# Four edits to the order of a hybrid decoder step: all samples of a head at once, a block's end in pieces, later recurrences, shifted query weights

## The chip, the cores and the metric

The kernel runs on one core of a Trainium2 chip. The metric is the device time of one execution in microseconds; the median of the runs counts. A core has TensorE (PE, with its weight loads as PEld), VectorE (DVE), ScalarE (ACT), GpSimd (POOL) and SyncE (SP, which here only issues transfers). Transfers are issued from SP, ACT and POOL.

## The reference

One layer of a decoder trunk for a prompt of 2048 tokens and eight single-token samples that carry state. All is float32.

```python
hn = rmsnorm(x, g_norm) * (1 + scale) + shift            # scale, shift, gate from silu(c) @ w_ada + b_ada
xa, za, q, k, v, glr, zg = split(hn @ w_in)
xc = conv4(xa)                                           # RG-LRU group, 8 blocks of 128 channels
gx, ga = sigmoid(xc @ w_gate_x + b_x), sigmoid(xc @ w_gate_a + b_a)
a = exp(8 * ga * log_sigmoid(lambda));  u = sqrt(1 - a**2) * gx * xc
h_t = a_t * h_{t-1} + u_t;              y_lru = h * silu(za)
S_t = diag(alpha_t) S_{t-1} + k_t^T v_t;  o_t = q_t S_t  # gated linear attention, 4 heads, 128 x 256 state
y_gla = rmsnorm(o) * silu(zg)
y = rmsnorm(x + gate * (concat(y_lru, y_gla) @ w_out), g_final)
```

The samples take one step of each recurrence from their own states (`state_lru_h`, `state_lru_conv`, `state_gla`), and the new states are outputs, for the attention eight matrices of 128 x 256 per head.

## The kernel before

**Arithmetic.** A float32 projection is done as three products of rounded parts (high x high, high x low, low x high), all at the rate of one product each; `hh` and `hl` hold the high and low part of the normalized input `hn`, channels on the partitions. Every weight tile holds its high and low part (`weights`); parts that were made once are kept in device memory (`parts`) and loaded again for the second half.

**Stages.** The prompt is worked in two halves of 1024 tokens; `SEGS` cuts a half into segments of 512 and 512 (first half) or 384, 384 and 264 columns (second half, the last 8 being the samples).

1. Start: the modulation from `w_ada`, `hn` of the first half, and the values, keys and queries of the first head (head 3). The tiles of this stage lie in the pool `start`, the first head's query weights `wq` among them.
2. First half: for each head of `HEADS` = (3, 0, 1, 2) `gla_head` and then `lru` for the RG-LRU blocks of `LRU_TILES`, here (0), (1, 2), (3, 4), (5, 6, 7). The last block, 7, is done in `lru_last_a`, where the normalization of the second half (`next_hn`) is dealt out among its projections (`drips`).
3. Middle: `gates_ahead` and `gates_seven` for the gates of the second half and `lru_seven` for blocks 0 and 1, products of 2 x 2 blocks done as seven (`seven`). Their operands are sums of quarters of `hn`, made on VectorE and ScalarE by `sums`, again dealt out by `drips`, two per product.
4. Second half: `gla_head(1, h)` and one block of `LATE_TILES` after each head, then blocks 6 and 7 while the first operands of the output projection are made (`early`).
5. Output projection, residual and the final norm, in an order written out by hand.

**Order.** Within the program text, work that belongs later is queued with `after(units, fn)` on a heap and run by `tick`; a unit is one projection of 512 columns, a product of `seven` is half a unit. The queued functions of the attention are flagged `gla`, its chunks also `val`; `new_values` runs what is queued before the value tiles are taken again, `flush_gla` everything of the attention. What stands where in each engine's queue is then decided by a planner: it goes through the instructions by the order in which they were written and by its own estimate of when their inputs are ready and their tile is free. `behind(q)` places what it encloses behind the last instruction written on that engine. A tile of a pool is named by its tag; each tag has a fixed number of buffers, and a new tile waits for the last user of the buffer that it takes. Here this concerns `xt` (two of 1032 columns in `xp`), `wr` (two of 1088 columns in `wp`, for raw weights), `zs` (four of 512 columns, for gate values), and the single tiles of an RG-LRU block: `xa` (the convolution's input), `cv` (its output), `xl`, `tx` and `tg`.

**The attention's recurrence.** `gla_qk` makes the scaled query and key of a segment; `chunks` starts the recurrence (`gla_start`, two tiles of products and transposes) and goes on chunk by chunk; `finish` normalizes, turns (`gla_out`) and gates with `zs`. In the second half `sample_state` and `sample_out` do the samples of a head in two groups of four: load values `vb` and states `s0` into two `xt` tiles, scale by the decay (ScalarE), add the outer product (VectorE), multiply by the queries laid out in `qm` (TensorE, `po`, each sample on its own 32 columns of the array), and store the states.

**An RG-LRU block.** `xa_unit` projects and convolves, `gates` multiplies by the gate weights, takes the tanh and, with the last segment, goes on to the block's end: the exponentials and the root on ScalarE, three products and the scan on VectorE. `za_unit` makes the gate; `out` multiplies and stores to `mixd`, from which the output projection reads.

Of the kernel before, what the change touches and what calls it, by code (L numbers as in the profile page):

```python
# [8 lines left out]
F32 = mybir.dt.float32  # L9
# [5 lines left out]
P = 128  # L15
# [34 lines left out]
def dram(ap, off, pattern):  # L50
    return bass.AP(tensor=ap.tensor, offset=ap.offset + off, ap=pattern)
# [3 lines left out]
def hybrid_kernel(ctx, tc, i, o):  # L55
# [381 lines left out]
    with tc.tile_pool(name="ada", bufs=1, side="right") as ap:  # L437
# [263 lines left out]
    def after(units, fn, gla=False, val=False):  # L701
        clock[1] += 1
        heapq.heappush(pend, (clock[0] + units, clock[1], fn, gla, val))
# [8 lines left out]
            heapq.heappop(pend)[2]()  # L712

    def flush_gla():
        while any(e[3] for e in pend):
            e = min(e for e in pend if e[3])
            pend.remove(e)
            heapq.heapify(pend)
            e[2]()

    def ada_gate():

# [365 lines left out]
        for c in range(nch):  # L1088
            V.tensor_scalar(on[:, c], on[:, c], rs[:, c:c + 1], None, op0=OP.mult)

    def sample_state(h, smp, b0, st, done):

        if b0 == 0:
            st[:] = [cp.tile([P, NS, 32], F32, tag="sc", name="qm"), gp.tile([P, DV], F32, tag="os", name="os")]
            V.memset(st[0], 0.0)
        qm = st[0]
        vb = xp.tile([P, 4, DV], F32, tag="xt", name="xt")
        G.dma_start(vb, dram(vsd, (h * NS + b0) * DV, [[0, P], [DV, 4], [1, DV]]))
        s0 = xp.tile([P, 4, DV], F32, tag="xt", name="xt")
        G.dma_start(s0, i["state_gla"][0, b0:b0 + 4, h].rearrange("b k v -> k b v"))  # L1100
        for n in range(4):
            b = b0 + n
            V.tensor_copy(qm[:, b, b:b + 1], smp[:, 0, b:b + 1])
            S.activation(s0[:, n], s0[:, n], AF.Copy, scale=smp[:, 2, b:b + 1])  # L1104
            V.scalar_tensor_tensor(s0[:, n], vb[:, n], smp[:, 1, b:b + 1], s0[:, n],
                                   op0=OP.mult, op1=OP.add)
        after(3, lambda: sample_out(h, b0, st, s0, done), True)

    def sample_out(h, b0, st, s0, done):

        qm, os_ = st
        po = psum.tile([P, 512], F32, tag="o", name="po", bufs=1)[:, :DV]
        for n in (3, 0, 1, 2):
            PE.matmul(po[32 * n:32 * n + 32], qm[:, b0 + n], s0[:, n], start=True, stop=True)
        G.dma_start(o[7][0, b0:b0 + 4, h].rearrange("b k v -> k b v"), s0)
        if b0 == 0:
# [7 lines left out]
        V.tensor_scalar(os_, os_, rs[:, :1], None, op0=OP.mult)  # L1124
        done()

    def silu(z, ps):
        S.activation(z, ps, AF.Tanh, scale=0.5)  # L1128
# [41 lines left out]
    def gla_head(half, h, wv=None, ahead=None):  # L1170
# [4 lines left out]
        else:  # L1175
# [8 lines left out]
        prep, zs, os_, state = {}, {}, [None], []  # L1184

        def chunks(s, c):

# [31 lines left out]
        def sample(smp, b0):  # L1219
            sample_state(h, smp, b0, state, lambda: after(0.5, lambda: os_.__setitem__(0, state[1]), True))  # L1220

        pk = None
        if not wv:
# [38 lines left out]
    def lru_units(half, last_a=None, seven=False):  # L1262
# [40 lines left out]
                V.tensor_tensor(xl[:, c], cv[:, c], xh[:, c].bitcast(F32), op=OP.subtract)  # L1303

        def gates(t, ss):
            j, cv, xh, xl, wgh, wgl, res = t.j, t.cv, t.xh, t.xl, t.wgh, t.wgl, t.res
            if ss[0] == 0:
                t.tx, t.tg = t_("tx"), t_("tg")
            tx, tg = t.tx, t.tg
            for s in ss:  # L1310
                c0, sn = t.segs[s]
                c = slice(c0, c0 + sn)
                for g, (out, bias) in enumerate(((tx, hbx), (tg, hba))):
                    ps = acc()[:, :sn]
                    PE.matmul(ps, wgh[:, g], xh[:, c], start=True, stop=False)  # L1315
                    PE.matmul(ps, wgh[:, g], xl[:, c], start=False, stop=False)
                    PE.matmul(ps, wgl[:, g], xh[:, c], start=False, stop=True)
                    S.activation(out[:, c], ps, AF.Tanh, bias=bias[:, j:j + 1], scale=0.5)  # L1318
            if ss[-1] < len(t.segs) - 1:
                return  # L1320
            n_ = slice(0, TH + (NS if t.samples else 0))
            a = last_a() if last_a else t_("xl")
            S.activation(a[:, n_], tg[:, n_], AF.Exp, bias=lc2[:, j:j + 1], scale=lc2[:, j:j + 1])

            S.activation(tg[:, n_], tg[:, n_], AF.Tanh, bias=lc4[:, j:j + 1], scale=lc4[:, j:j + 1])
            S.activation(tg[:, n_], tg[:, n_], AF.Sqrt, scale=0.25)
            if half == 1 and j in LRU_TILES[3][:2]:

                S.activation(t.one, tg[:, :1], AF.Tanh)
            V.scalar_tensor_tensor(tx[:, n_], tx[:, n_], 1.0, cv[:, n_], op0=OP.add, op1=OP.mult)  # L1330
            V.scalar_tensor_tensor(tg[:, n_], a[:, n_], 1.0, tg[:, n_], op0=OP.add, op1=OP.mult)
            V.tensor_tensor(tx[:, n_], tx[:, n_], tg[:, n_], op=OP.mult)
            h = tg
            V.tensor_tensor_scan(h[:, pr], a[:, pr], tx[:, pr], 0.0 if half == 0 else hc[:, j:j + 1],  # L1334
                                 op0=OP.mult, op1=OP.add)
            if half == 0:
                V.tensor_copy(hc[:, j:j + 1], h[:, TH - 1:TH])
            else:
                V.tensor_copy(stT[:, j, 3:4], h[:, TH - 1:TH])
            if t.samples:  # L1340
                V.tensor_tensor(h[:, sm], a[:, sm], vecT[:, j, R_H0:R_H0 + NS], op=OP.mult)
                V.tensor_tensor(h[:, sm], h[:, sm], tx[:, sm], op=OP.add)
                V.tensor_copy(stT[:, j, 12:20], h[:, sm])
            res.append(h)

        def out(t, s, z):
            j, h = t.j, t.res
            if not h:
                after(1, lambda: out(t, s, z))
                return  # L1350
            c0, sn = t.segs[s]
            V.scalar_tensor_tensor(z, h[0][:, c0:c0 + sn], 0.5, z, op0=OP.mult, op1=OP.mult)
            spill(z, j, half, c0, sn)
# [24 lines left out]
        def xa_new(t):  # L1378
            t.xh = t_("xh", F32R, 48)
            t.one = lp.tile([P, 1], F32, tag="one", name="one")  # L1380
            t.xl, t.xa, t.cv = t_("xl", F32R), t_("xa", extra=8), t_("cv")
            if half == 0:
                V.memset(t.xa[:, :3], 0.0)
            else:
                V.tensor_copy(t.xa[:, :3], xac[:, t.j])
# [21 lines left out]
        def za_unit(t, s):  # L1407
            c0, sn = t.segs[s]
            z = xp.tile([P, 512], F32, tag="f512", name="z5") if half == 1 and t.j == LRU_TILES[3][0] and s == 2 else None
            z = silu2(t.wz, c0, sn, z)  # L1410
            after(2, lambda: out(t, s, z))
            tick()

        if seven:
            return xa_load, xa_new, xa_unit, out
        return xa_load, xa_unit, za_load, za_unit

    def lru(half, js, wx=None):
# [205 lines left out]
        seven(n, use, lambda s: new(), n == 0)  # L1624

    def lru_seven(j):
        xa_load, xa_new, xa_unit, out = lru_units(1, seven=True)
# [12 lines left out]

    def gates_ahead(h):

# [616 lines left out]
```

## Time and profile before

| | |
|---|---|
| runs | 1453.64, 1453.55, 1456.39 us (median 1453.64) |
| profiled execution | 1452.05 us |
| its span, first to last instruction | 1450.3 us |
| granted TensorE clock | 0.997 of full speed |
| busy: TensorE, weight loads, VectorE, ScalarE, GpSimd | 1425.6, 1253.1, 1051.2, 690.0, 220.5 us |
| transfers | 305.33 MB, 211 GB/s in the mean |

The profile is that of one execution; its own time, not the median, is what its rows add up to. A row of the timeline gives the start, the duration, engine, line, operation and tiles of one instruction or of a few merged ones (x), and in brackets the idle time of the engine before it and what ended it. `PE ... <- DVE ...` in the list of waits means that TensorE idled until that VectorE instruction was done. Matmuls overlap: a busy time of 0.39 us and a distance of 0.23 us to the next are both right.

### The profile page before, as it was taken

The page shows a single profiled execution, that of the slowest core. Times are in us where ns is not written, and L with a number is a line of the kernel's source. Part 1 is how long each engine was busy: PE and PEld are TensorE (multiplying, and loading weights), DVE is VectorE, ACT ScalarE, POOL GpSimd, SP SyncE. Part 2 cuts the span into 40 slices and gives each one's busy share as a digit, 9 for nine tenths or more (in the row PEclk, how much of TensorE's full clock was granted, in tenths as well). Part 3 has the DMA queues.
Part 4 walks back from the last instruction along what each step waited for, and adds up shares of the span by engine and source line. Part 5 has one row for each costly group of instructions (what it writes and reads, how often), then busy time and mean ns, then how long its engine had stood idle before and what let it go on. Part 6 is the DMA issues. An engine that isn't in the chain of part 4 may idle for free. (4 is left out here: it accounts for less than half of the span.)

```text
span 1450.3 us, 23579 instructions
## 1 busy us (share of the span) xinstructions
PE 1425.6 (98%) x8741; PEld 1253.1 (86%) x8741; DVE 1051.2 (72%) x2477; ACT 690.0 (48%) x1251; POOL 220.5 (15%) x364
## 2 busy tenths in 40 slices
PE   8999999999999999999999999999999999999998
PEld 6888989899898988878999998999998887788886
DVE  5757658776676688955458687686888986688886
ACT  4644544662545358624354544535557522144342
POOL 0200111212122013100111321433210000000000
PEclk9999999999999999999999999999999999999999
DMA  9755775774665446667844665756672767694453
GB/s 329 267 185 175 259 264 196 251 243 156 200 217 192 160 175 213 204 224 236 293 153 154 201 205 163 244 188 203 213 256 77 279 223 273 229 361 135 135 173 116
DMA packets 161752, 305.33 MB, mean 211 GB/s; under 512 B 12962, under 2 KB 91458, under 8 KB 159197
## 3 DMA queue, kind: packets, MB, share of 16 engines
q1 hardware_dynamic: 106837, 217.39, 44.0%
q0 software_dynamic: 22752, 70.44, 14.3%
q10 hardware_dynamic: 32048, 16.00, 3.7%
q8 instruction: 69, 1.13, 0.3%
q14 instruction: 46, 0.38, 0.1%
HBM read 188.51 MB, written 115.33 MB: 210 GB/s over the span
## 5 line engine op out<-in xcount | busy, mean ns | idle before, releaser
L661 PE MATMUL acc<-hh,w 128*128 128x512 f32 (+3 forms) x1112 | 386.2, 347 | 1.3 <-DVE zs L1129 0.7
L663 PE MATMUL acc<-hh,w 128*128 128x512 f32 (+3 forms) x1112 | 375.6, 338 | 0.0
L662 PE MATMUL acc<-hl,w 128*128 128x512 f32 (+3 forms) x1112 | 375.3, 338 | 0.2 <-DVE hl L205 0.2
L661 PEld LDWEIGHTS acc<-hh,w 128*128 128x128 f32 x1112 | 209.3, 188 | 20.0 <-ACT tx L1318 0.9
L662 PEld LDWEIGHTS acc<-hl,w 128*128 128x128 f32 x1112 | 209.3, 188 | 17.2 <-DVE hl L205 0.5
L663 PEld LDWEIGHTS acc<-hh,w 128*128 128x128 f32 x1112 | 209.1, 188 | 16.8 <-issue 0.4
L1845 PE MATMUL acc<-w,a 128*128 128x512 f32 (+1 forms) x792 | 184.8, 386 | 0.0
L1845 PEld LDWEIGHTS acc<-w,a 128*128 128x128 f32 x792 | 146.8, 188 | 33.2 <-issue 3.4
L346 PE MATMUL acc<-w,hh 128*128 128x256 f32 (+1 forms) x508 | 144.9, 285 | 0.1
L347 PE MATMUL acc<-w,hh 128*128 128x256 f32 (+1 forms) x508 | 143.6, 283 | 0.0
L348 PE MATMUL acc<-w,hl 128*128 128x256 f32 (+1 forms) x508 | 143.6, 283 | 0.0
L1845 PE MATMUL tp<-w,a 128*128 128x512 f32 x564 | 136.0, 391 | 0.0
L1845 PEld LDWEIGHTS tp<-w,a 128*128 128x128 f32 x564 | 105.3, 188 | 26.8 <-issue 5.2
L346 PEld LDWEIGHTS acc<-w,hh 128*128 128x128 f32 x508 | 96.8, 191 | 1.3 <-ACT zs L1128 0.4
L348 PEld LDWEIGHTS acc<-w,hl 128*128 128x128 f32 x508 | 96.4, 190 | 0.0
L347 PEld LDWEIGHTS acc<-w,hh 128*128 128x128 f32 x508 | 95.9, 189 | 0.2
L1128 ACT ACTIVATE zs<-acc 128x512 f32<-128x512 f32 (+3 forms) x70 | 34.5, 492 | 107.4 <-PE acc L663 105.2
L1695 ACT CAST a<-s 128x512 fp32r<-128x512 f32 x61 | 36.5, 619 | 95.9 <-issue 36.6
L1278 DVE SCALAR_TENSOR_TENSOR cv<-xa,vecT,cv 128x512 f32<-128x512 f32 (+2 forms) x120 | 77.1, 645 | 6.0 <-ACT cv L1276 5.7
L1129 DVE SCALAR_TENSOR_TENSOR zs<-zs,acc 128x512 f32<-128x512 f32 (+3 forms) x70 | 38.6, 551 | 47.3 <-ACT zs L1128 47.2
L957 ACT CAST vh<-acc 128x256 fp32r<-128x256 f32 x56 | 20.5, 370 | 83.3 <-PE acc L348 70.0
L958 DVE TENSOR_TENSOR vl<-acc,vh 128x256 fp32r<-128x256 f32 x56 | 23.4, 420 | 43.1 <-ACT vh L957 43.0
(403 smaller groups left out, 2752.0 us busy)
## 6 DMA issues: line engine op xcount, KB each, us to landing
parts<-w SPq DMA_DIRECT2D x37, 1024.0 KB
w<-parts SPq DMA_DIRECT2D x28, 1024.0 KB
wr<-in_w_in_dram SPq DMA_DIRECT2D x38, 512.0 KB
a<-mixd SPq DMA_DIRECT2D x63, 256.0 KB
w<-wd SPq DMA_DIRECT2D x12, 1024.0 KB
w<-twd SPq DMA_DIRECT2D x20, 512.0 KB
mixd<-zs ACTq DMA_DIRECT2D x34, 256.0 KB
wada<-in_w_ada_dram SPq DMA_DIRECT2D x16, 512.0 KB
```

The source lines that it names most:

```text
L346: PE.matmul(ps, hh[:, kt, c], hi[:, kt % 4], start=kt == 0, stop=False)
L347: PE.matmul(ps, hh[:, kt, c], lo[:, kt % 4], start=False, stop=False)
L348: PE.matmul(ps, hl[:, kt, c], hi[:, kt % 4], start=False, stop=kt == KT - 1)
L661: PE.matmul(ps[:, :n], hi[:, kt], a, start=kt == 0, stop=False)
L662: PE.matmul(ps[:, :n], hi[:, kt], b, start=False, stop=False)
L663: PE.matmul(ps[:, :n], lo[:, kt], a, start=False, stop=kt == KT - 1)
L958: V.tensor_tensor(lo, ps[:, :DV], hi.bitcast(F32), op=OP.subtract)
L1128: S.activation(z, ps, AF.Tanh, scale=0.5)
L1129: V.scalar_tensor_tensor(z, z, 1.0, ps, op0=OP.add, op1=OP.mult)
L1278: V.scalar_tensor_tensor(cv[:, cq], xa[:, cq.start + k:cq.stop + k], cw[k], cv[:, cq], op0=OP.mult, op1=OP.add)
L1695: S.copy(t[:, 0, k], (low(t) if src is None else src)[:, k])
L1845: PE.matmul(ps, t[:, u, k], w[:, v, k, c], start=(q < 3 or ps is own) and (k, u, v) == (0, 0, 0), stop=(k, u) == (3, 1), skip_group_check= ...
```

## The change

Four edits, independent in the code:

- **Query weights.** The tile of the first head's query weights gets 56 columns more, and the weights are placed behind them.
- **Recurrences.** In the first half the recurrence of heads 0, 1 and 2 starts two units after the first `gla_qk` instead of one (head 3 had two already). `flush_gla` sets the clock to the due time of what it runs, so that what is queued from there is queued from that time, and sets it back at its end.
- **The end of block 7 in the first half.** The end of a block becomes a list of four functions, `chain`: exponentials, root and first product; second product; third product; scan. They are run at once for every other block; for block 7 of the first half they are run 4.5, 5, 5.5 and 6 units after its gates, each behind the last VectorE and ScalarE instruction written by then. `out` looks for the result every half unit. The gate values of this block go into the columns of its `xa` tile instead of `zs` tiles. `lru_seven` fills the first columns of its `xa` only before its first sum into it (`xa_first`).
- **Samples.** `sample_state` loads and updates all eight samples, 0 to 3 in two `xt` tiles, 4 to 7 in two `wr` tiles; four units later (instead of three for each group) `sample_out` does all their matmuls, the second four added to the first in `po`, and stores. One copy takes the place of a copy and an add.

```diff
-        wkq0.append(weights(Q0 + HEADS[0] * DK, DK, both=st.tile([P, 2, D], F32R, name="wq"), later=True))
+        wkq0.append(weights(Q0 + HEADS[0] * DK, DK, both=st.tile([P, 2 * D + 56], F32R, name="wq")[:, 56:].rearrange("p (j n) -> p j n", j=2), later=True))
...
     def flush_gla():
+        now = clock[0]
         while any(e[3] for e in pend):
...
+            clock[0] = max(now, e[0])
             e[2]()
+        clock[0] = now
...
-    def sample_state(h, smp, b0, st, done):
...
+    def sample_state(h, smp, done):
+
+        qm = cp.tile([P, NS, 32], F32, tag="sc", name="qm")
+        V.memset(qm, 0.0)
+        s0 = []
+        for b0, pool, tag in ((0, xp, "xt"), (4, wp, "wr")):
+            vb, x = [pool.tile([P, 1088], F32, tag=tag, name=tag)[:, :4 * DV] if b0 else
+                     pool.tile([P, 4 * DV], F32, tag=tag, name=tag) for _ in range(2)]
+            vb, x = [y.rearrange("p (b v) -> p b v", v=DV) for y in (vb, x)]
+            G.dma_start(vb, dram(vsd, (h * NS + b0) * DV, [[0, P], [DV, 4], [1, DV]]))
+            G.dma_start(x, i["state_gla"][0, b0:b0 + 4, h].rearrange("b k v -> k b v"))
+            for n in range(4):
...
+            s0.append(x)
+        after(4, lambda: sample_out(h, qm, s0, done), True)
+
+    def sample_out(h, qm, s0, done):
+
+        os_ = gp.tile([P, DV], F32, tag="os", name="os")
         po = psum.tile([P, 512], F32, tag="o", name="po", bufs=1)[:, :DV]
-        for n in (3, 0, 1, 2):
-            PE.matmul(po[32 * n:32 * n + 32], qm[:, b0 + n], s0[:, n], start=True, stop=True)
-        G.dma_start(o[7][0, b0:b0 + 4, h].rearrange("b k v -> k b v"), s0)
-        if b0 == 0:
-            V.tensor_copy(os_, po)
-            return
-        V.tensor_tensor(os_, os_, po, op=OP.add)
+        for m in range(2):
+            for n in (3, 0, 1, 2):
+                PE.matmul(po[32 * n:32 * n + 32], qm[:, 4 * m + n], s0[m][:, n], start=m == 0, stop=m == 1)
+        for m in range(2):
+            G.dma_start(o[7][0, 4 * m:4 * m + 4, h].rearrange("b k v -> k b v"), s0[m])
+        V.tensor_copy(os_, po)
...
-                after(2 if h == HEADS[0] else 1, lambda: chunks(0, 0), True, True)
+                after(2 if half == 0 or h == HEADS[0] else 1, lambda: chunks(0, 0), True, True)
...
-            after(1, lambda: sample(prep[2][3], 0), True)
-            after(3, lambda: sample(prep[2][3], 4), True)
+            after(1, lambda: sample(prep[2][3]), True)
...
+            if half == 0 and j == LRU_TILES[3][-1]:
+
+                def late(ops):
+                    with behind(V), behind(S):
+                        ops[0]()
+                    if ops[1:]:
+                        after(0.5, lambda: late(ops[1:]))
+                after(4.5, lambda: late(chain(t)))
+            else:
+                for f in chain(t):
+                    f()
+
+        def chain(t):
...
+            return [rates, scale, inputs, scan]
...
-                after(1, lambda: out(t, s, z))
+                after(0.5 if half == 0 and j == LRU_TILES[3][-1] else 1, lambda: out(t, s, z))
...
+            if half == 0 and t.j == LRU_TILES[3][-1]:
+                z = t.xa[:, c0:c0 + sn]
...
-        seven(len(HEADS) - 1 + j, use, lambda s: t.xa[:, 3 + s * 512:3 + s * 512 + 512])
+        def c2(s):
+            if s == 0:
+                xa_first(t)
+            return t.xa[:, 3 + s * 512:3 + s * 512 + 512]
+
+        seven(len(HEADS) - 1 + j, use, c2)
```

More of the change, by code (lines that the diff above doesn't have):

```diff
@@ L1089, in gla_norm @@
             V.tensor_scalar(on[:, c], on[:, c], rs[:, c:c + 1], None, op0=OP.mult)
-    def sample_state(h, smp, b0, st, done):
-        if b0 == 0:
[L1094 to L1107, printed above, removed]
@@ L1109, in sample_out @@
[L1109 to L1119 removed]
+    def sample_state(h, smp, done):
[9 more added lines that the diff above has]
+            for n in range(4):
+                b = b0 + n
+                V.tensor_copy(qm[:, b, b:b + 1], smp[:, 0, b:b + 1])
+                S.activation(x[:, n], x[:, n], AF.Copy, scale=smp[:, 2, b:b + 1])
+                V.scalar_tensor_tensor(x[:, n], vb[:, n], smp[:, 1, b:b + 1], x[:, n],
+                                       op0=OP.mult, op1=OP.add)
+            s0.append(x)
+        after(4, lambda: sample_out(h, qm, s0, done), True)
@@ L1124, in sample_out @@
         V.tensor_scalar(os_, os_, rs[:, :1], None, op0=OP.mult)
-        done()
+        done(os_)
     def silu(z, ps):
@@ L1217, in finish, with sample @@
             gla_out(half, h, s, prep[s, "run"][1], os_[0] if s == 2 else None, [zs[s, 0], zs[s, 1]])
-        def sample(smp, b0):
-            sample_state(h, smp, b0, state, lambda: after(0.5, lambda: os_.__setitem__(0, state[1]), True))
+        def sample(smp):
+            sample_state(h, smp, lambda x: after(0.5, lambda: os_.__setitem__(0, x), True))
         pk = None
@@ L1321, in gates @@
             n_ = slice(0, TH + (NS if t.samples else 0))
             a = last_a() if last_a else t_("xl")
[L1323 to L1344, printed above, removed]
+            def rates():
+                S.activation(a[:, n_], tg[:, n_], AF.Exp, bias=lc2[:, j:j + 1], scale=lc2[:, j:j + 1])
+                S.activation(tg[:, n_], tg[:, n_], AF.Tanh, bias=lc4[:, j:j + 1], scale=lc4[:, j:j + 1])
+                S.activation(tg[:, n_], tg[:, n_], AF.Sqrt, scale=0.25)
+                if half == 1 and j in LRU_TILES[3][:2]:
+                    S.activation(t.one, tg[:, :1], AF.Tanh)
+                V.scalar_tensor_tensor(tx[:, n_], tx[:, n_], 1.0, cv[:, n_], op0=OP.add, op1=OP.mult)
@@ new lines, in scale, with inputs, scan @@
+            def scale():
+                V.scalar_tensor_tensor(tg[:, n_], a[:, n_], 1.0, tg[:, n_], op0=OP.add, op1=OP.mult)
+            def inputs():
+                V.tensor_tensor(tx[:, n_], tx[:, n_], tg[:, n_], op=OP.mult)
+            def scan():
+                h = tg
+                V.tensor_tensor_scan(h[:, pr], a[:, pr], tx[:, pr], 0.0 if half == 0 else hc[:, j:j + 1],
+                                     op0=OP.mult, op1=OP.add)
+                if half == 0:
+                    V.tensor_copy(hc[:, j:j + 1], h[:, TH - 1:TH])
+                else:
+                    V.tensor_copy(stT[:, j, 3:4], h[:, TH - 1:TH])
+                if t.samples:
+                    V.tensor_tensor(h[:, sm], a[:, sm], vecT[:, j, R_H0:R_H0 + NS], op=OP.mult)
+                    V.tensor_tensor(h[:, sm], h[:, sm], tx[:, sm], op=OP.add)
+                    V.tensor_copy(stT[:, j, 12:20], h[:, sm])
+                res.append(h)
@@ L1381, in xa_new, with xa_first @@
             t.xl, t.xa, t.cv = t_("xl", F32R), t_("xa", extra=8), t_("cv")
+            if not seven:
+                xa_first(t)
+        def xa_first(t):
             if half == 0:
@@ L1414, in lru_units @@
         if seven:
-            return xa_load, xa_new, xa_unit, out
+            return xa_load, xa_new, xa_first, xa_unit, out
         return xa_load, xa_unit, za_load, za_unit
@@ L1626, in lru_seven @@
     def lru_seven(j):
-        xa_load, xa_new, xa_unit, out = lru_units(1, seven=True)
+        xa_load, xa_new, xa_first, xa_unit, out = lru_units(1, seven=True)
         t = xa_load(j, [None])
```

6 lines of the change are left out of this document (4 added, 2 removed).

## The prediction

> **What bounds the kernel now.** I read the page's engine shares first, then busy time by stage, then TensorE's own waits.
>
> ```profile
> span 1450.3 us, 23579 instructions
> ...
> PE 1425.6 (98%) x8741; PEld 1253.1 (86%) x8741; DVE 1051.2 (72%) x2477; ACT 690.0 (48%) x1251; POOL 220.5 (15%) x364
> ```
>
> ```profile
> 602.20:627.20 25.00, 22.73 (x97) 17.72 (x96) 22.36 (x26) 9.80 (x13) 1.14 (x2) 1.00 0.69 225
> 1059.50:1125.90 66.40, 62.46 (x401) 59.05 (x400) 55.01 (x127) 45.65 (x78) 4.83 (x7) 1.00 0.46 152
> 1125.90:1438.10 312.20, 312.20 (x1397) 248.72 (x1397) 247.96 (x405) 114.48 (x212) 2.73 (x4) 1.00 0.62 220
> ```
>
> TensorE is the bound: it idles 1450.3 - 1425.6 = 24.7 us of the span. From 1125.9 us to 1438.1 us it never idles at full clock (columns: PE, PEld, DVE, ACT, POOL, clock), so whatever is saved ahead of 1125.9 us arrives at the end whole. No edit removes projection work; the change can only close holes, and the holes have names:
>
> ```profile
> PE po L1114 <- DVE xt L1105: 2.1, 1, 2.1
> ...
> PE acc L1559 <- DVE so L1495: 1.4, 2, 1.2
> PE acc L1315 <- DVE zs L1129: 1.4, 1, 1.4
> PE acc L1315 <- ACT tx L1318: 1.1, 1, 1.1
> PE tp L1042 <- DVE xb L1027: 1.0, 1, 1.0
> PE tp L1164 <- DVE os L1124: 0.8, 1, 0.8
> PE acc L1559 <- DVE ra L1495: 0.8, 1, 0.8
> PE tp L1162 <- DVE on L1089: 0.7, 1, 0.7
> PE acc L661 <- DVE zs L1129: 0.7, 1, 0.7
> ```
>
> (Columns: us in total, times, longest.) These are one-off misplacements: a step stands in TensorE's queue before its input is there. The four edits aim at the first two, the fifth to the seventh and perhaps the eighth. A row shows idle time only; the step after a hole also loses its overlap with the one before it, 0.16 us, as the next rows show (0.39 us long, started every 0.23 us).
>
> **Query weights.** Offset alone changes, by 56 elements.
>
> ```profile
> 56.93 0.40 PE L661 MATMUL acc<-hh,wq 128*128 128x512 f32 x1
> ...
> 59.49 0.40 PE L663 MATMUL acc<-hh,wq 128*128 128x512 f32 x1
> ...
> 74.66 0.39 PE L661 MATMUL acc<-hh,w 128*128 128x512 f32 x1
> ...
> 77.83 0.39 PE L663 MATMUL acc<-hh,w 128*128 128x512 f32 x1
> ```
>
> Between the first two rows lie 11 starts, 2.56 / 11 = 0.233 us each; between the last two, with any other weight tile, 14 starts, 3.17 / 14 = 0.226 us. The query tile serves 48 matmuls: 48 x 0.0063 = -0.3 us, if the offset is the cause; otherwise 0, and the tiles placed behind it move by 224 bytes and could lose as much, +0.3. I take -0.3, the like tiles' pace. [...]
>
> **First-half recurrences a unit later.** A unit is one 512-column projection, 24 x 0.226 = 5.4 us. Three heads move; the first had two units already.
>
> ```profile
> 188.25 0.69 DVE L1027 SCALAR_TENSOR_TENSOR xb<-acc,xb 128x512 f32<-128x512 f32 x1
> ```
>
> This product feeds the recurrence's first matmuls (L1042), which are queued straight behind the projection and waited 1.0 us for it. A unit later they stand behind the next key projection, 5.4 us on: -(1.0 + 0.16) = -1.2. The hole at L1162 (norm late) keeps its distance from the last chunk, but meets another set of VectorE work: between -0.9 and +0.9, I take -0.4. The gated outputs leave 5.4 us later; the four gate tiles they hold are next wanted by the RG-LRU's gate units, two or three convolution units on, so I cost that at nothing; without that cover each head's next silu slips, at most by the same unit. The recurrences' flush now advances the clock; by the unit counts nothing is pending at the first flush, and at the second the sample step is already out, so 0.
>
> **The last first-half block in four pieces.**
>
> ```profile
> 575.22 0.75 DVE L1278 SCALAR_TENSOR_TENSOR cv<-xa,vecT,cv 128x512 f32<-128x512 f32 x1
> ...
> 577.24 0.69 DVE L1129 SCALAR_TENSOR_TENSOR zs<-zs,acc 128x512 f32<-128x512 f32 x1
> ...
> 595.34 1.22 DVE L1330 SCALAR_TENSOR_TENSOR tx<-tx,cv 128x1024 f32<-128x1024 f32 x1
> ...
> 601.02 1.22 DVE L1331 SCALAR_TENSOR_TENSOR tg<-xl,tg 128x1024 f32<-128x1024 f32 x1
> ...
> 602.75 1.22 DVE L1332 TENSOR_TENSOR tx<-tx,tg 128x1024 f32<-128x1024 f32 x1
> ...
> 605.02 2.29 DVE L1334 TENSOR_TENSOR_SCAN tg<-xl,tx 128x1024 f32<-128x1024 f32 x1
> ...
> 607.86 1.29 DVE L1352 SCALAR_TENSOR_TENSOR zs<-tg,zs 128x512 f32<-128x512 f32 x2
> ...
> 628.65 0.69 DVE L1129 SCALAR_TENSOR_TENSOR zs<-zs 128x512 f32<-128x512 f32 x1 [0.94 <-ACT zs L1128]
> ```
>
> In the window 602.2 to 627.2 VectorE is busy 22.4 of 25.0 us: there it, not TensorE, sets the pace. Ahead of the sums stand 1.22 + 1.22 + 1.22 + 2.29 + 1.29 = 7.2 us of this block. Behind the sums they are off that path, and the three holes at L1559 (1.4 + 0.8 idle, three starts) close: -(2.2 + 3 x 0.16) = -2.7. ScalarE loses its exp, tanh and root from the same stretch.
>
> Two waits come in. The second gate's tanh now writes into the convolution's own input tile, so it waits for the convolution's last read at 575.22 + 0.75 = 576.0 us; modulation steps queue behind it, and the hole at L661 (0.7, ended by the silu of 577.24) hangs on it. Between 0 and +0.8 (a tanh of these 512 columns, put at the 0.69 of the silu's other step, ends at 576.7, still ahead of 577.24): +0.2. And that tile stays taken until both outputs are stored.
>
> ```profile
> 608.58 1.10 ACTq L675 DMA_DIRECT2D mixd<-zs  x2
> ```
>
> ```profile
> 635.44 0.39 PE L1559 MATMUL acc<-hh,w 128*128 128x512 f32 x1
> ```
>
> ```profile
> zgd<-zs POOLq DMA_DIRECT2D x4, 256.0 KB, 4.3
> ```
>
> The scan stands behind the last silu of the first gate block, 628.65 + 0.69 = 629.3, less the 2.7 that TensorE is ahead: 626.6. Add scan 2.3, outputs 1.3, issues 1.1, landing 4.3 (the like-sized store): 635.6. Then the first sum into the tile (0.7) ends at 636.3, and the T3 product, which overwrites what that sum reads, is due at 635.44 - 2.7 = 632.7. That is up to 3.6 us late; but the B21 product needs neither and fills 12 x 0.226 = 2.7. So +0.9, between 0 and +3.6. Behind the waiting sum on VectorE stand the next convolution and its gates, which have a unit of slack. [...]
>
> **Eight samples at once.**
>
> ```profile
> 833.53 0.77 POOL L1100 DMA_DIRECT2D xt<-in_state_gla_dram  x1
> ...
> 879.94 0.76 POOL L1100 DMA_DIRECT2D xt<-in_state_gla_dram  x1
> ```
>
> ```profile
> 878.18 0.64 PE L1114 MATMUL po<-xt,qm 128*32 128x256 f32 x8
> ...
> 887.34 0.89 PE L1114 MATMUL po<-xt,qm 128*32 128x256 f32 x8 [2.12 <-DVE xt L1105]
> ...
> 1060.06 0.64 PE L1114 MATMUL po<-xt,qm 128*32 128x256 f32 x8
> 1060.63 0.45 PE L661 MATMUL acc<-hh,w 128*128 128x384 f32 x1
> ```
>
> ```profile
> 885.01 1.71 ACT L1104 ACTIVATE xt<-xt,smp 128x256 f32<-128x256 f32 x4 [2.06 <-DMA xt<-in_state_gla_dram]
> ```
>
> Samples 0 to 3 are loaded 45 us before their matmuls. Samples 4 to 7 reuse the tiles: their load goes out after the first burst (878.18, 879.94), ScalarE stands 2.06 us for it, TensorE 2.12. With tiles of their own both loads go out near 834: -(2.1 + 0.2) = -2.3. In the last head the same lateness ends in the wait at L1164: -(0.8 + 0.2) = -1.0. A burst takes 1060.63 - 1060.06 = 0.57 us, of which about half is the work of eight matmuls and half the change of shape; one burst of sixteen for two of eight saves 4 x 0.3 = -1.2 (0 to -2.3). VectorE loses one add per head. In the last head, four scalings and four updates leave the stretch from 1059.5, where VectorE is busy 55 of 66 us and ends the waits of 1.4 and 1.1 at L1315: -1.0, between 0 and -2.5.
>
> Against that: per head four ScalarE scalings (1.71 us) and four updates, put at as much VectorE, move up beside the first four samples', among the recurrence whose chain runs through both engines. At most 1.7 us x 4 = 6.8 if nothing hides them, 0 if all is hidden; VectorE is 72% busy and the planner prefers what is written earlier, here the recurrence, so I take +1.5. Four loads in a row instead of two also hold POOL's queue; what stands behind them there are the output weights' combinations, which are wanted in the last stage.
>
> **Sum.** -0.3 - 1.2 - 0.4 - 2.7 + 0.2 + 0.9 - 2.3 - 1.0 - 1.2 - 1.0 + 1.5 = -7.5 us. The profiled execution took 1452.05 us (1450.3 span and 1.75 around it): 1444.6. The median shown is 1.6 higher, 1453.64, so 1446.1 on that scale.
>
> **Rivals.** *Holes move, none closes (no change).* The order of the instructions is computed from estimated durations; every edit reorders it, and the crowding of samples costs its bound of 6.8 us rather than 1.5: -7.5 + 5.3 = -2.2, 1451.4 (to 1454.5 with the T3 wait and the tanh at their bounds as well, +2.7 and +0.6). For it: the holes above are such misplacements. Against: three of the four edits lengthen the distance to a step's input. One gain not arriving (the T3 wait at its 3.6 bound, -7.5 + 2.7) is 1448.8, inside my forecast.
>
> *The input queue blocks (slower).* Samples 4 to 7 take the two raw-weight tiles.
>
> ```profile
> 1003.37 1.03 SPq L1960 DMA_DIRECT2D wr<-mixd  x2
> ```
>
> ```profile
> 1033.00 0.52 SPq L293 DMA_DIRECT2D w<-parts  x1
> ```
>
> ```profile
> 1051.28 0.33 PE L661 MATMUL acc<-hh,w 128*128 128x384 f32 x1
> ```
>
> In the last head SP loads the output stage's first operands into these tiles at 1003.37. After the change the tiles are free only after the burst, now at 1060.06 to 1060.63. If SP's order still has those loads ahead of the weight load of 1033.00, whose gate projection starts at 1051.28, that weight lands at 1060.6 + 1.0 + 0.5 + 4.3 = 1066.4 and TensorE stands 15.1 us: 1461.2. It decides as soon as the loads stand ahead of any weight that is used before 1066. Against it: they are written last in the program, so a planner that knows the tile is taken puts them later. On POOL the same tiles delay the next head's raw values by a store; the eight value projections stand ahead of their use.
>
> *The second four are still late (not what it says).* If the loads stay after 880, the 2.3 and 1.0 remain: 1449.4, inside the range.
>
> **Numbers.** Forecast 0.66 (with the late-load case and the single miss inside it), likeliest 1446.1; no change 0.17; slower by the queue 0.1; 0.07 left for several new holes at once that outweigh the gains, some +4. Forecast bounds: below, no crowding (-1.5), no T3 wait (-0.9) and half of what the burst and the last head may still give (-1.3) make 1442.4; above, the T3 wait (+2.7), the norm (+1.3) and the tanh (+0.6) at their bounds make 1450.7. Up to 1454.5 the no-change case is in; the slow one is left out. Faster by over 0.2% (2.9 us, about what this kernel's measurement can tell) 0.66, within 0.17, slower 0.17.
>
> **What would show it.** Right: no wait above 0.5 us at what L1114 and L1164 become; one burst of sixteen per head; no wait for VectorE's sums; the recurrence's first transposes of head 0 without a wait; query matmuls at 0.226 us. Wrong: TensorE waiting at the second seven-product block for a sum into the convolution tile, SP standing behind the loads of L1960, or new waits at the recurrences' starts in the second half.

## The result

The change makes the kernel 0.18% faster: a median of 1450.85 us over 22 runs against 1453.43 us over 22 runs of the kernel before, ratio 0.9982 with a 95% interval of 0.9976 to 0.9989. That is 2.6 us where 7.5 were forecast. The one execution that was profiled took 1455.26 us, the longest of the 22, so its total (span 1453.5 us) says nothing of the gain; its stages can be read one by one.

TensorE runs as many matmuls as before (8741) and is as busy (1425.6 us there), so what can differ is idle time and clock:

```profile
span 1453.5 us, 23570 instructions
...
PE 1425.4 (98%) x8741; PEld 1253.5 (86%) x8741; DVE 1052.1 (72%) x2473; ACT 690.0 (47%) x1251; POOL 220.4 (15%) x364
```

TensorE's waits in the changed kernel (engine and line, what ended the wait; total, times, longest):

```profile
PE acc L1592 <- DVE xa L1601: 4.4, 1, 4.4
...
PE acc L661 <- DVE S L1059: 2.0, 1, 2.0
...
PE pkv L1073 <- DVE kTl L1055: 1.5, 4, 0.7
...
PE acc L1318 <- DVE zs L1133: 1.4, 1, 1.4
PE po L1075 <- DVE on L1084: 1.0, 2, 0.7
...
PE tp L1168 <- DVE os L1128: 0.6, 2, 0.4
```

Against the list of before: the waits of the sample matmuls (2.1), of the recurrence's first transposes (1.0), for the sums `so` and `ra` (2.2) and for the norm at L1162 (0.7) are gone. In their place stands one of 4.4 us, at the product of the second seven-product block that waits for its sum into `xa`, the T3 product of the prediction (`product(y, ZT3, ...)` in `seven`; the first of the RG-LRU's). Busy time by stretch around it (PE, PEld, DVE, ACT, POOL, then the granted clock):

```profile
602.20:627.20 25.00, 25.00 (x111) 20.35 (x110) 21.04 (x23) 16.11 (x20) 1.58 (x3) 1.00 0.76 247
634.77:639.17 4.40, 0.01 (x1) 0.00 (x0) 0.80 (x2) 0.00 (x0) 0.00 (x0) 1.00 0.90 284
639.17:642.90 3.73, 3.73 (x9) 2.95 (x10) 2.19 (x3) 0.81 (x1) 0.00 (x0) 0.54 0.04 17
642.90:646.60 3.70, 3.70 (x18) 3.04 (x17) 2.63 (x5) 1.84 (x3) 0.00 (x0) 1.00 0.00 0
```

The first row is the stretch in which VectorE set the pace before: TensorE is now busy for all of its 25.0 us (22.73 before). The next rows are the bill. TensorE idles 4.40 us, and then runs 3.73 us at a granted clock of 0.54 (half clock, in what follows): 9 matmuls there against 18 in the like stretch that follows, some 1.7 us lost on top (3.73 x 0.46). How the wait arises, in the same trace:

```profile
628.43 2.28 DVE L1359 TENSOR_TENSOR_SCAN tg<-xl,tx 128x1024 f32<-128x1024 f32 x1
...
630.82 1.28 DVE L1379 SCALAR_TENSOR_TENSOR xa<-tg,xa 128x512 f32<-128x512 f32 x2
...
631.53 0.97 ACTq L675 DMA_DIRECT2D mixd<-xa  x2
...
638.32 0.17 DVE L1416 COPY xa<-xac 128x3 f32<-128x3 f32 x1 [6.22 <-DMA mixd<-xa]
638.43 0.69 DVE L1601 TENSOR_TENSOR xa<-acc,es 128x512 f32<-128x512 f32 x1
...
639.17 0.59 PE L1592 MATMUL acc<-hh,w 128*128 128x512 f32 x1 [4.40 <-DVE xa L1601]
```

Scan, outputs, two stores issued at 631.5, both landed by 638.3; only then may the next block write into that tile.

### The profile page after: what moved, and what is told of

It reads as the page before. It is cut to its first block, busy times and chain, and to the rows that moved or that the text cites. A ratio compares the mean times of both kernels' runs of the same rounds, so it can differ in the third digit from the quotient of the medians.

```text
span 1453.5 us, 23570 instructions
## 1 busy us (share of the span) xinstructions
PE 1425.4 (98%) x8741; PEld 1253.5 (86%) x8741; DVE 1052.1 (72%) x2473; ACT 690.0 (47%) x1251; POOL 220.4 (15%) x364
## 4 chain that ended last, share of the span: by engine, by line
PE 80%; DVE 9%; ACT 4%; issue 3%; DMA 2%; SPq 1%; POOL 1%; ACTq 0%; DVEq 0%; POOLq 0%
PE acc L1883 12%; PE acc L661 11%; PE acc L663 11%; PE acc L662 11%; PE tp L1883 9%; PE acc L1592 6%; PE acc L346 3%; PE acc L347 3%; PE acc L348 3%; PE po L1079 2%; PE acc L1318 1%; PE tp L1166 1%; PE acc L1320 1%; PE acc L1319 1%; DVE cv L1281 1%
```

## The experiments

Ratios are to the kernel before, from runs on the same chip; an interval is one of 95%. The difference of two ratios carries both intervals, so a difference between two variants is good to some 2 to 3 us; what is smaller rests on the traces.

**The block's end as before.** All the code of that edit is undone, the rest of the change stays.

```diff
-                after(4.5, lambda: late(chain(t)))
...
+            for f in chain(t):
+                f()
...
-            if half == 0 and t.j == LRU_TILES[3][-1]:
-                z = t.xa[:, c0:c0 + sn]
```

> The changed kernel with the end of block 7 put back as it was before (at once, gate values in their own tiles); samples, recurrences and query weights stay changed. Theory (the block's edit gave its gain back at the T3 product: 4.4 us idle and then 3.4 us at half clock, some 1.7 us more): that 6.1 goes, the three waits for sums come back with some 2.7 to 3, so about 3 us under the changed kernel, 5.7 under the kernel before (1447.7), and no TensorE wait over 1 us at the second seven-product block. Rival (the T3 wait belongs to the one profiled execution, the loss is elsewhere): the edit is worth its predicted -1.6, and the time rises to about 1.0 under the kernel before (1452.4).

Measured: 1448.89 us, ratio 0.9969 (0.9957 to 0.9982): faster than the whole change by 0.13%, 1.9 us, though the two intervals overlap. The T3 wait is gone; the waits for sums are back:

```profile
617.02 1.67 PE L1580 MATMUL acc<-so,w 128*128 128x512 f32 x6 [1.21 <-DVE so L1516]
...
620.43 0.50 PE L1580 MATMUL acc<-ra,w 128*128 128x512 f32 x1 [0.82 <-DVE ra L1516]
```

So this edit, forecast at -2.7 + 0.2 + 0.9 = -1.6, costs some 1.9 as it stands. The theory holds, with a size under its 3, and the rival (1.0 us under the kernel before) is out.

**Two groups of samples again.** `sample_state`, `sample_out` and their calls as in the kernel before.

```diff
...
-            after(1, lambda: sample(prep[2][3]), True)
+            after(1, lambda: sample(prep[2][3], 0), True)
+            after(3, lambda: sample(prep[2][3], 4), True)
```

> The changed kernel with the samples in two groups of four again; the other three edits stay. Theory (the samples' edit gains what its stages show, 5.6 us in the second half when the 2.0 us wait at 921.8 and the half clock behind it are taken out as that execution's own late weight load): about 3.0 us over the kernel before (1456.4), with the wait of 2.1 us for the second four back. Rival (the crowding of eight samples beside the recurrence, and loads in a row ahead of the next weights, eat most of it; the 921.8 wait is theirs): the edit is worth 2 us or less, so about 0.6 us under the kernel before (1452.8) or lower.

Measured: 1455.69 us, ratio 1.0015 (1.0003 to 1.0026). The samples' edit is worth 0.33%, 4.8 us: the largest gain of the four, and the rival is out.

```profile
PE po L1117 <- issue: 2.3, 2, 1.6
...
PE tp L1167 <- DVE os L1127: 0.9, 1, 0.9
PE acc L1318 <- ACT tx L1321: 0.9, 1, 0.9
```

The waits come back where the prediction had them: for the second four samples (twice, 1.6 us at the longest), for their norm, and in the last head's stretch.

**Recurrences a unit earlier.** The clock of `flush_gla` is undone too.

```diff
...
-                after(2 if half == 0 or h == HEADS[0] else 1, lambda: chunks(0, 0), True, True)
+                after(2 if h == HEADS[0] else 1, lambda: chunks(0, 0), True, True)
```

> The changed kernel with the first half's recurrences of heads 0, 1 and 2 one unit after the first scaled query again, and the flush as before. Theory (the edit is worth the 1.2 us of one wait and nothing else): 1.2 us over the changed kernel (1.4 under the kernel before, 1452.0), with the wait of 1.0 us at head 0's first transposes back. Rival (the later unit moves work onto other waits and costs 1 us or more in sum): the same or lower than the changed kernel.

Measured: 1450.85 us, ratio 0.9981 (0.9970 to 0.9991), no different from the change's 0.9982. The times show neither the 1.2 nor a loss. The traces say the same more sharply: from head 0's first decay product (L976 in the change, L973 here) to the `hl` product near 597 us lie 420.5 us in the change and 420.8 here. The edit is worth next to nothing. Its trace, against that of the change, shows how. Without the edit (first fence) head 0 has both old waits; with it (second fence) one new wait stands in the recurrence's first chunk.

```profile
188.88 1.16 PE L1042 MATMUL tp<-xb,e 128*128 128x128 f32 x8 [0.96 <-DVE xb L1027]
...
225.40 1.14 PE L1163 MATMUL tp<-ident,on 128*128 128x128 f32 x8 [0.47 <-DVE on L1089]
```

```profile
202.65 0.38 PE L1073 MATMUL pkv<-vh,kTl 128*128 128x256 f32 x1 [0.72 <-DVE kTl L1055]
```

**Query weights at offset 0.**

```diff
...
-st.tile([P, 2 * D + 56], F32R, name="wq")[:, 56:].rearrange("p (j n) -> p j n", j=2)
+st.tile([P, 2, D], F32R, name="wq")
```

> The changed kernel with the query weights at offset 0; the order of the instructions is the same on every engine, so that this is also a second trace of the changed kernel. Query products go back from 0.227 to 0.233 us each, 0.3 us over the changed kernel (2.3 under the kernel before), too little for the times to tell. Theory on the rest: the wait at the T3 product of the second block is there again, 3 to 4.5 us with some 3 us at half clock behind it, and the wait of 2.0 us at 921.8 is not (a weight load that landed late once). Rival: the T3 wait is below 2 us here, or the 921.8 wait is there too and so belongs to the order.

Measured: 1450.89 us, ratio 0.9986 (0.9976 to 0.9997); the times can't tell 0.3 us. The pace can. Eight starts in the changed kernel (first fence) and in this one (second):

```profile
54.70 0.39 PE L663 MATMUL acc<-hh,wq 128*128 128x512 f32 x1
...
56.51 0.39 PE L662 MATMUL acc<-hl,wq 128*128 128x512 f32 x1
```

```profile
53.44 0.40 PE L663 MATMUL acc<-hh,wq 128*128 128x512 f32 x1
...
55.31 0.40 PE L662 MATMUL acc<-hl,wq 128*128 128x512 f32 x1
```

1.81 / 8 = 0.226 with the 56 columns in front, 1.87 / 8 = 0.234 without. So the offset is the cause, and the prediction's other case, by which this term is 0, is out. With the same order of instructions this is also a second trace of the change: the T3 wait is there (3.3 us), the wait at 921.8 is 0.3 us.

**Two pieces instead of four.** The scan goes with the second piece and so some 7 us earlier.

```diff
-                        after(0.5, lambda: late(ops[1:]))
+                        after(0.5, lambda: late([lambda: [f() for f in ops[1:]]]))
```

> The changed kernel with the end of block 7 in two pieces: exponentials, root and first product 4.5 units after the gates as now; second and third product and scan together half a unit later, so that the scan stands some 6 us earlier on VectorE. Theory (the T3 product waits because the block's two stores are issued 3 to 4 us too late for their 6 us to landing): the T3 wait (2.7 to 4.4 us in the four traces with it) and the half clock behind it (1.7 us) go, at most 1.2 us comes back at the first block's T3 product, whose sum now shares VectorE with the scan; 4 us under the changed kernel, 6.5 under the kernel before (1446.5). Rival (the wait hangs on the traffic of the weights at that place, which slows any store there): the wait stays over 2 us and the time within 1 us of the changed kernel.

Measured: 1446.58 us, ratio 0.9948 (0.9934 to 0.9962). Theory: 4 us under the change, measured 4.9 by the ratios. The T3 wait is gone; 1.3 us came back at the first block's T3 product, as the theory allowed.

```profile
624.46 1.28 DVE L1379 SCALAR_TENSOR_TENSOR xa<-tg,xa 128x512 f32<-128x512 f32 x2
...
633.59 0.17 DVE L1416 COPY xa<-xac 128x3 f32<-128x3 f32 x1 [5.32 <-DMA mixd<-xa]
```

The stores take longer here (issued from 625.17, landed by 633.6), but they start in time, so the rival is out.

**Gate values in the gate tiles, pieces kept.** One statement less than the change:

```diff
-            if half == 0 and t.j == LRU_TILES[3][-1]:
-                z = t.xa[:, c0:c0 + sn]
```

> The changed kernel with one line taken out: block 7's gate values stay in two of the four gate tiles, as before the change, so that its convolution tile is free once the convolution has read it; the late pieces stay. Theory (the tile held for the stores makes the T3 wait): the T3 wait is gone entirely; two gate tiles are taken some 20 us longer, and the gates of the next head, which take six tiles in a row, may wait for them by up to the same 3 to 5 us; between 1446 and 1451.5. Rival (the late pieces themselves delay the first sum on VectorE and ScalarE): the T3 wait stays at 2 us or more.

Measured: 1445.70 us, ratio 0.9947 (0.9932 to 0.9961). The stores are issued at 636.4 here, later than in the change, and nobody waits for them. What is left at this place is 0.8 us (second row); the first row is a wait at 580 us that the kernel before had with 0.7:

```profile
PE acc L661 <- DVE zs L1133: 1.1, 1, 1.1
...
PE acc L1590 <- DVE xa L1599: 0.8, 1, 0.8
```

The feared wait for gate tiles didn't come. So it is the held tile, not the late pieces, that made the T3 wait.

**The idle time filled.** Twelve matmuls that nobody reads, ahead of T3.

```diff
...
+            with behind(PE):
+                for _ in range(12):
+                    PE.matmul(po, hh[:, 0, :P], hh[:, 0, :512], start=True, stop=True)
         product(y, ZT3, n, False)
```

> The changed kernel with twelve matmuls of 512 columns whose result nobody reads put ahead of the T3 product where TensorE waits (12 x 0.227 = 2.7 us of work that fills the wait). Theory (the 3.4 us at half clock follow from the idle time): TensorE resumes at T3 when it did, without half clock; 1.7 us under the changed kernel where that had the half clock, 1 to 1.7 in the median (about 1449.4), although the work is more. Rival (the half clock does not come from the idle time): it stays in the trace, and the time is that of the changed kernel or up to 0.5 us higher.

Measured: 1449.80 us, ratio 0.9970 (0.9957 to 0.9983): 1.7 us under the change by the ratios, with more work; the intervals overlap, so the gain in time isn't clear of noise. The clock stays up:

```profile
634.40:637.00 2.60, 1.44 (x7) 0.90 (x6) 0.96 (x3) 0.00 (x0) 0.00 (x0) 1.00 0.96 299
637.00:640.40 3.40, 3.40 (x16) 2.77 (x16) 2.45 (x4) 0.81 (x1) 0.00 (x0) 1.00 0.28 108
```

Of the wait, 1.16 us are left, and no half clock follows. One trace alone would be weak, since the kernel without the recurrences' edit has none either behind 2.7 us; the last section sets idle time beside the clock records. By these rows the half clock follows from idle time, and it is a cost of its own beside it (1.7 us in the change).

**B21 ahead of T3.** The order that the prediction had assumed.

```diff
+        if early:
+            product(x, ZB21, n, False)
+            use(0, 0, x)
         product(y, ZT3, n, False)
...
+            if not early:
+                product(x, ZB21, n, False)
+                use(0, 0, x)
...
```

> The changed kernel with the B21 product of the second seven-product block (the first of the RG-LRU) ahead of the T3 product instead of behind it, the order that the prediction took for the T3 wait. Theory (the prediction's 0.9 us failed because the order was fixed and B21 did not fill): 2.7 us of the wait are filled, 0.6 is left, no half clock; about 4.3 us under the changed kernel, 6.9 under the kernel before (1446.1). Rival (B21's own operands or its silu come late in this order): a wait of 2 us or more at B21 or T4, and the time within 1.5 us of the changed kernel.

Measured: 1450.91 us, ratio 0.9981 (0.9970 to 0.9993), no gain; a miss for the theory. B21 did fill, but T4, the next product into the same sum, then follows T3 directly and stands for the second sum into `xa`, from which B21 had kept it apart:

```profile
638.33 0.50 PE L1592 MATMUL acc<-hh,w 128*128 128x512 f32 x1 [1.38 <-DVE xa L1601]
...
644.31 0.50 PE L1592 MATMUL acc<-hh,w 128*128 128x512 f32 x1 [2.04 <-DVE xa L1601]
```

3.4 us of idle time in two parts. The trace shows no half clock at this place, so by it 1 to 2 us should have been left as a gain; the times don't show it. They can't exclude it either (some 2 us to either side), and the 2.04 us could bring half clock in other executions; that stays open.

**Without the recurrences' edit, on the better base.** The variant with the gate values in the gate tiles, with the edit of the recurrences undone as above.

> The variant with block 7's gate values in the gate tiles and the late pieces, but with the first half's recurrences one unit after the scaled query as before the change. Theory (the recurrences' edit closes two waits of 1.33 and 0.82 us at head 0 and gives them back: some 0.6 to 1.1 at a new wait for the low key part, 0.4 and 0.2 at heads 1 and 2 where the turning matmuls now follow the chunks directly): no difference beyond 0.5 us, within 0.1% of that variant, near 1445.5. Rival (the edit is worth its predicted 1.6 us and the earlier run without it hid that behind a shorter T3 wait): 1.6 us slower than that variant, 1447.3.

Measured: 1446.06 us, ratio 0.9949 (0.9933 to 0.9965) against 0.9947 with the edit. Again nothing, free of the T3 wait this time. The times alone couldn't exclude 1.6 us; the same stretch of the traces can: 420.6 us with the edit, 420.05 without. The forecast of 1.6 was wrong.

**Gate tiles and two pieces together.**

> The variant with block 7's gate values in the gate tiles, and the end in two pieces: exponentials, root and first product 4.5 units after the gates, the rest half a unit later. Theory (what is left there is one wait of 0.8 us for the second block's first sum, which stands behind the scan, against one of 1.3 us for the first block's first sum when the scan comes earlier): the two exchange, no gain beyond 0.5 us; 1445.2 to 1446.7. Rival (both waits close, since neither the store nor the scan is on the way any more): 0.9 us faster, 1444.8.

Measured: 1448.55 us, ratio 0.9966 (0.9953 to 0.9979), by the ratios slower than either alone, though the intervals overlap; neither theory had that. ScalarE's and TensorE's rows:

```profile
624.52 0.97 ACTq L675 DMA_DIRECT2D mixd<-zs  x2
629.77 0.63 ACT L1132 ACTIVATE zs<-zs 128x512 f32<-128x512 f32 x1 [5.28 <-DMA mixd<-zs]
630.31 0.58 ACT L1604 COPY acc<-acc 128x512 f32<-128x512 f32 x1
```

```profile
621.10 0.50 PE L1590 MATMUL acc<-hh,w 128*128 128x512 f32 x1 [1.21 <-DVE zs L1599]
...
630.94 3.46 PE L1590 MATMUL acc<-so,w 128*128 128x512 f32 x13 [1.35 <-ACT acc L1604]
```

With the stores moved ahead of a silu in ScalarE's order, that silu's gate tile is the one that the stores hold: the same mechanism, 5.28 us on ScalarE and 1.35 on TensorE, in another tile. Of this trace's time 2.2 us more (and half clock behind it) belong to a late weight load near 918, below.

## Why the prediction missed its size

Most of the terms came near, the largest (samples) and the sums' waits above all. One failed in its mechanism, and another was worth nothing.

- **T3 wait, forecast +0.9: measured about +5.** This is the step that failed. The wait itself was foreseen: without cover the prediction's sum gives 3.6 us, and the four traces with the held tile and this order have 4.4, 3.3, 3.3 and 2.7. What was wrong is the cover: it took off 2.7 us for a B21 product that the program's order puts behind T3, and when B21 is put ahead of T3, T4 loses its distance to the second sum instead. And there was no price for the clock: 3.4 us at half clock, 1.7 us, behind the wait of 4.4 us (none behind the one of 2.7). The landing was not the fault: from the first issue to the landing of both stores the prediction had 1.1 + 4.3 = 5.4 us, and these traces have 6.8, 5.7, 5.7 and 5.1. By the ratios the late pieces are worth 0.9947 / 0.9969, -3.2 us, when no tile is held, and +1.9 when it is: 5.1 between the two.
- **Sums' waits, forecast -2.7: right.** -3.2 us with the tile free.
- **The tanh's place, forecast +0.2.** It belongs to the held tile and is inside the 5.1. From head 2's second decay product to the `hl` product near 597 us the change takes 146.07 us, the variant with the gate tiles 145.81: +0.3.
- **Recurrences, forecast -1.6: measured 0, twice.** The waits at L1042 and L1162 closed, the second further than the 0.4 put for it. Moved by a unit, the first chunk's product with the low key part waits for VectorE (0.72 us, 0.99 in a second trace), and at heads 1 and 2 the turning matmuls now stand directly behind the chunks, without idle time: at head 1 the step from the last chunk to them takes 0.67 us, against 0.25 from that chunk to other work without the edit. The prediction looked at the step that it moved and not at the next ones of the chain.
- **Samples, forecast -4.0: measured -4.8.** One burst of sixteen per head with no wait. The first burst in the change, and one of eight among like matmuls in the kernel before:

```profile
798.73 0.28 PE L663 MATMUL acc<-hh,w 128*128 128x264 f32 x1
798.95 0.64 PE L1120 MATMUL po<-xt,qm 128*32 128x256 f32 x8
799.40 0.61 PE L1120 MATMUL po<-wr,qm 128*32 128x256 f32 x8
...
800.18 0.28 PE L662 MATMUL acc<-hl,w 128*128 128x264 f32 x1
```

```profile
795.61 0.28 PE L663 MATMUL acc<-hh,w 128*128 128x264 f32 x1
795.82 0.64 PE L1114 MATMUL po<-xt,qm 128*32 128x256 f32 x8
...
796.62 0.28 PE L1316 MATMUL acc<-xl,wg 128*128 128x264 f32 x1
```

  The matmul ahead of a burst and the one behind it also take longer to the next start than the 0.12 us that is usual here, so a burst is counted from the first row of a fence to its last, less two usual steps: 1.45 - 0.24 = 1.21 us for sixteen, 1.01 - 0.24 = 0.77 for eight. That is 2 x 0.77 - 1.21 = 0.33 per head, the 0.3 of the forecast. The wait at L1164 fell from 0.8 to 0.4, not to nothing; in the last head's stretch the 1.1 us at L1315 for `tx` is gone and the 1.4 for `zs` stays, the -1.0 of the forecast. In the kernel before, half clock followed the wait for the second four (rows below), a cost beyond its 2.1 us that the forecast did not have. Some crowding came too: the second half's recurrences wait 0.7 us or less at a time at `kTl` and `on`, 1.8 us in sum, where the forecast had put 1.5 for it.
- **Query weights, forecast -0.3: the pace agrees** (48 x 0.007).
- **The input queue** (rival, slower): it cost nothing, though its condition came about in part. SP does stand behind the second of the two loads until the burst is out, one of the prediction's signs of being wrong, but the weights behind it are not late; TensorE never idles on a weight in the last head.

```profile
SPq L1998 <- PE po L1120: 14.0, 1, 14.0
```

Added up with what the runs show: -0.3 + 0 + 1.9 - 4.8 = -3.2 for a measured -2.6, inside what the intervals leave. Had the gate values stayed in their tiles, the change would have given 1445.7 (ratio 0.9947, -7.7 us), nearly the forecast's -7.5; that version beats both kernels. The closeness is partly luck: the recurrences' 1.6 never came, and larger gains of the sums and the samples stand in for it.

One wait more came with the change: 2.0 us at 921.83 in head 1 of the second half. The list names a VectorE step that ends then, but the trace has the landing of the weight load (`w<-parts`, issued at 911.58) in 16 parts: thirteen are there by 919.20, the last at 921.70, and TensorE's weight load starts at 921.80. In the kernel before, TensorE's weight load starts at this place 0.1 us behind the last part of the same load too (919.26 behind 919.15), 8.3 us behind its issue at 910.92; in the change it is 10.2. The wait is 2.2 us in the last variant, 0.3 in the kernel with the weights at offset 0 and at most 1.1 in the rest (none without the late pieces); the kernel before and the one with two groups of samples have none, which speaks for a cost of the samples' edit, already inside its -4.8. What delays the last parts in some executions stays open.

## What to carry to other kernels

Putting a result into a tile that is free "until the block ends" lengthens that tile's life to the landing of the store (631.5 to 638.3 us here); price it from issue to landing as measured in that stretch, against the next writer, and count no other work as cover unless the order in the queue really puts it there. A late piece of work is safe when what it holds isn't the next thing wanted: one statement decided between some +1.9 and -3.2 us. When a chain is moved to close one wait, follow every later link of it to its next reader.

## What was not expected of the hardware

A wait of TensorE can cost 1.7 us beyond its idle time, and its length alone doesn't decide whether it does. First the kernel before, with its wait of 2.12 us for the second four samples (up to 887.34); then the last variant, behind 2.16 us at 918.53; then the kernel without the recurrences' edit, with 2.68 us up to 636.45:

```profile
884.18:887.59 3.41, 1.29 (x15) 1.01 (x15) 1.68 (x4) 1.71 (x4) 0.00 (x0) 1.00 0.26 43
887.59:891.00 3.41, 3.41 (x21) 2.84 (x14) 1.95 (x4) 1.74 (x5) 0.77 (x1) 0.50 1.00 408
```

```profile
918.53:921.90 3.37, 3.37 (x11) 3.37 (x12) 1.76 (x3) 0.66 (x2) 2.09 (x4) 0.50 0.39 125
```

```profile
632.12:635.54 3.42, 1.65 (x8) 1.02 (x6) 0.00 (x0) 0.00 (x0) 0.00 (x0) 1.00 0.97 271
635.54:638.95 3.41, 2.50 (x11) 2.10 (x12) 2.33 (x5) 0.82 (x1) 0.00 (x0) 1.00 0.78 284
```

Two waits of some 2.1 us were followed by 3.4 us at half clock, one of 2.7 us was not. The clock records of the kernel before and of the change, laid beside their idle time, show more. In each of the two, every start of half clock between 10 and 1440 us lies a whole number of steps of 3.413 us from every other: in the change at 11.39, 25.04, 639.44 and 922.75 us, 4, 180 and 83 steps apart ((922.75 - 11.39) / 267 = 3.413); in the kernel before at 24.02 and 887.59, 253 apart. Cut into stretches of this length that start there, the two traces have from 20 us on five stretches with 1.94 us of idle time or more (1.94 and 2.12 in the kernel before; 1.94, 3.14 and 2.01 in the change), and each is followed by one at half clock; no other has more than 1.37 us, and none of those is. Ahead of 20 us one stretch of the change, with 1.54 us, is followed by half clock too. The 2.12 us of the kernel before lay within one stretch, 884.18 to 887.59; the 2.68 us fell across two, 1.77 + 0.91 (third fence).

An estimate from these numbers, for 20 us and later: a single wait of up to some 1.8 us (1.77) doesn't cost the extra 1.7 us, one over 3.9 (2 x 1.94) does, and between them it hangs on where the wait falls in the stretches, and that differs between the two executions (half clock at 24.02 in the one, at 25.04 in the other). The start of the kernel differs too: up to 40 us the clock records of the kernel before have one stretch at half clock (24.02), those of the change two (11.39 and 25.04), though the two kernels differ only later, so that the totals of two profiled executions can differ by 1.7 us (3.41 x 0.50) for that reason alone.

The other surprise is how long 256 KB stores take to land beside weight loads: 5.1 to 6.8 us from the first issue to the landing of both in the four traces with the held tile, 8.4 in the kernel with two pieces, for a pair that is issued within 1 us.
